# A decoder layer on one core: softmax tiles per head, output casts ahead of their remainders, sines moved into the query round, and other places for w_in's and w_out's products

## The chip, the cores and the metric

The kernel runs on one core of a Trainium2 chip. The metric is the time of one execution on the device, in microseconds (us), as the median of several runs. The profile shows one further execution, whose own time is given beside its span.

## What is computed

The reference is one step of a hybrid decoder layer, in float32, for a prompt of 272 positions (16 meta tokens and 256 tokens) and 8 sample tokens that share the weights (`T` = 280 columns in all). Cut to what matters:

```python
h = rmsnorm(x, norm_mix_g)
z = h @ w_in                                   # 2048 -> u 1024 | q 1024 | k 256 | v 256
q = rope(rmsnorm(q, q_norm_g), pos); k = rope(rmsnorm(k, k_norm_g), pos)
# SSM: 64 groups of 16 channels, 64 complex states each
x_re, x_im = coef * (u @ b)                    # complex product per group
s = associative_scan(a, x)                     # s[t] = a * s[t-1] + x[t]
y = gelu(Re(s @ c) + d_skip * u);  y = y * sigmoid(y @ w_glu + b_glu)
# attention: 16 query heads on 4 key heads of 64, window 128, softmax with a sink per head
o = softmax([q @ k.T * 64**-0.5 | sink])[..., :-1] @ v   # prompt in blocks of 128;
                                               # each sample token against its 128 cached keys and itself
x = x + [rmsnorm(y) | rmsnorm(o)] @ w_out
x = x + (silu(gate) * val) @ w_down            # val, gate = conv3(rmsnorm(x) @ w_up), 5632 channels each
```

The outputs are the layer's result, the last 128 keys and values, the last SSM state, and the last rows of the convolution. The a of the scan needs a cosine and a sine of lam_im x dt, and the kernel also needs the cosines and sines of its multiples by the position within a chunk: these are the tiles `csT` and `snT`.

## The kernel before

Every product with a weight matrix is made as three products (`mm3`, L232 to L235): the weights and the activations are split into a high part in a shorter format and the remainder, and wh x xh, wh x xl and wl x xh add up in one accumulator `acc`. Weights come in blocks of 512 KB on SP's DMA queue (`wload`, L207 to L210, three buffers `w`). `wsplit` (L212) makes the two parts: ACT casts `wh` (L216), DVE subtracts `wl` (L72). Both have two buffers and go ahead of other work that is ready (`high_priority`), so the cast of block n waits until PE is done with block n - 2, and stands in ACT's order wherever the scheduler put it.

PE's order is the order of the program text; a scheduler sets the order of the other engines when the kernel is built. All engines run their instructions in that fixed order, and an engine whose next instruction waits does nothing else. The order of the program is made of generators that are advanced one step at a time with `next`:

- The query round (L747 to L753): 16 steps of `qs_`, half of a query product each (q1 to q8; q8a and q8b are the halves of the last). Between them run steps of `kv_chain` (keys) and of `prm`, which prepares the parameters of the SSM on DVE. The squares of each query product (`sqr_s`, L640, ACT) are summed by PE (`qss`, L724).
- `q_norm`, then the attention rounds i = 1 to 8 (L1016 to L1034). Each prompt group (`att_group`, L833 to L890; 4 key heads in blocks A, then B) has three steps: scores on PE (`sps`) and the softmax on DVE and ACT (maximum, exponentials `P`, L861, sum, reciprocal, scaled `P`, L867); transposes of P on PE (`ppt`, L875) and their copies `pt`; and the product with v (`ops`, L884) with `att_out` (L806 to L822), which writes the attention output as a cast `ah` (ACT, L814) and a remainder `al` (DVE, L815), and its squares `osqt` (ACT). I number them `sps0` to `sps7`, and `ppt` and `ops` likewise.
- Between the steps of the groups stand halves of the products for u (`us`, named U1, U2 and so on here; 24 matmuls each), steps of the attention of the meta tokens (`att_meta`: `mps`, `mtp`, `mop`) and of the sample tokens (`att_sample`, L892 to L955: `ssp` twice, `osp`, `otp`). Two tables say how many stand where in each round: `UD` for the halves of u (before the `ppt` of the round, after it, after `ops`), and `SD` for steps of meta and sample (before `ppt`, after `ops`); `side` (L1006) takes meta first.
- In the sample attention the cached keys come in four tiles `KT` of 256 KB on SP's queue (L901), with three buffers; POOL copies the new key into each (L902). `ssp1` reads the first two, `ssp2` the other two.
- Before round 1, `prm_trig` makes `csT` and `snT` on ACT in four slices: an `Abs` (L451), a cosine (L452) and a sine (L453) each.

Behind the rounds stands the loop over eight state-space units, with halves of w_out's products (`oas`, 12 matmuls each) between its steps. Unit i is prepared by `ssm_in` (`lps`, L1082 to L1090), its taps by `ssm_fir`; then `vps` (L1115), the rotation `z`, `q` on DVE with `csT` and `snT`, the scan (L1129) with the factors `d0`, and the output `yps`. `d0` (L1061) is made once, from `mg4` and `mask`. The sums of squares of the attention output (`ors_`: `orps`, then a reciprocal square root on DVE, then `dg` and a second `orps`, which spreads it over the partitions) scale what w_out gives for the attention half (`oas<-acc,ors`). The gate of the SSM, the rest of w_out and the convolutional FFN follow; from 345 us on the FFN's products run one behind the other.

Of the kernel before, what the change touches and what calls it, by code (L numbers as in the profile page):

```python
# [65 lines left out]
def body(ctx, tc, I, O, dbg=None):  # L66
# [132 lines left out]

    UD = ((1, 1, 0), (2, 1, 0), (1, 1, 0), (0, 2, 0), (0, 1, 1), (1, 1, 0), (0, 1, 0), (0, 0, 0))  # L200

    SD = ((1, 0), (1, 1), (1, 1), (1, 1), (1, 1), (1, 0), (0, 1), (1, 1))

# [67 lines left out]
    def run(g):  # L271
        for _ in g:
            pass
# [316 lines left out]
    sp = pool(ssm_ctx, "ssm", "right")  # L590
    SO = sp.tile([128, 2, 9, 32], F32, name="SO")
    csT = sp.tile([128, 32, 80], F32, name="csT")
# [4 lines left out]
    ah0 = sp.tile([128, 2, 32, 8], F32, name="ah0")  # L597
    mask = sp.tile([128, SC_], F32, name="mask")
    sdp = sp.tile([128, 8], F32, name="sdp")
    V.memset(mask, 1.0)  # L600
    V.memset(mask[:, 0:1], 0.0)
    V.memset(mask[:, NCH:SC_], 0.0)
    G.tensor_copy(sdp, vsl("ssm_d"))
# [140 lines left out]
    for f in range(4):  # L744
        A.copy(kvr[:, f, :], kv_ps[f])
    kvc = kv_chain()
    for i in range(16):  # L747
        next(qs_)
        if i < 2:
            next(rs1)  # L750
        if i > 0:
            next(kvc, None)
        if i >= 2:  # L753
            slices(prm, 1)
    run(kvc)
    run(prm)
# [52 lines left out]
    def att_out(f, src, c, n):  # L809

        m = src.shape[1]
        for a in range(m):
            g = vcol("attn_out_g", f + a)
            A.activation(ah[:, f + a, c:c + n], src[:, a], AF.Copy, scale=g)  # L814
            V.scalar_tensor_tensor(al[:, f + a, c:c + n], src[:, a], g, ah[:, f + a, c:c + n].bitcast(F32),  # L815
                                   op0=OP.mult, op1=OP.subtract)
        z = small.tile([128, T], F32, name="osqt", tag="tb")[:, :m * n].rearrange("p (a b) -> p a b", a=m)
        A.activation(z, src, AF.Square)
        o = osq[:, c:c + n]
        if f == 0:  # L820
            add(o, z[:, 0], z[:, 1], eng=G)
        for a in range(2 if f == 0 else 0, m):  # L822
            add(o, o, z[:, a], eng=G)
# [11 lines left out]
    def att_group(nm, kv):  # L835
# [22 lines left out]
        add(se, sk, nm_)  # L858
        P = aw.tile([128, 4, 256], F32, name="P", bufs=1)
        for r in range(4):  # L860
            A.activation(P[:, r, :nk], sps[:, r % 2, r // 2, :nk], AF.Exp, scale=sc[:, r:r + 1], bias=nm_[:, r:r + 1],  # L861
                         accum_out=den[:, r:r + 1])
# [3 lines left out]
        for r in range(4):  # L866
            A.activation(P[:, r, :nk], P[:, r, :nk], AF.Copy, scale=rec[:, r:r + 1])  # L867
        hp.__exit__(None, None, None)
# [4 lines left out]
        for bi, (c, n, vv) in enumerate(blocks):  # L873
            for r in range(4):
                PE.transpose(ppt[:n, bi, r, :], P[:, r, c:c + n], ident)  # L875
        for bi, (c, n, vv) in enumerate(blocks):
# [128 lines left out]
    def side(k):  # L1005
        for _ in range(k):  # L1006
            if next(mg, 1) == 1:
# [3 lines left out]
                   oa_evac(f), step=4, hold=True) for f in range(16)]  # L1011
    trig = prm_trig()
    slices(trig, 4)
    next(gs_[0])
    next(us)
    next(gs_[0])  # L1016
    for i in range(1, 9):
        if i < 8:
            next(gs_[i])
        for _ in range(UD[i - 1][0]):  # L1020
            next(us)
        side(SD[i - 1][0])
        next(gs_[i - 1])
        if i < 8:
# [4 lines left out]
        if i == 8:  # L1029
            run(mg)  # L1030
            run(sg)
            next(oas[0])
        next(gs_[i - 1])
# [19 lines left out]
    for t in (*C0s, *kzs):  # L1053
        G.memset(t, 0.0)
    SO4 = SO.rearrange("p c b r -> p c r b")
    Li, U2, FIR, lpk = {}, {}, {}, {}
# [120 lines left out]
    ssm_load(0)  # L1177
    next(oas[0])
    ssm_in(0)
    next(oas[1])  # L1180
    next(ors_)
    ssm_load(1)
# [276 lines left out]
```

## Time and profile before

| | |
|---|---|
| median of 3 runs | 1163.37 us (1162.06 to 1163.4) |
| the profiled execution's own time | 1162.89 us |
| its span, from the first to the last instruction | 1161.1 us |
| mean granted clock of TensorE | 0.991 |
| PE busy | 1119.5 us (96% of the span), 9479 instructions |
| DVE busy | 807.0 us (69%) |
| ACT busy | 584.7 us (50%) |
| POOL busy | 88.2 us (8%) |
| HBM | 204 MB moved, 176 GB/s over the span |

Busy time is a sum over the whole span. The engine PE is the array of TensorE, DVE VectorE, ACT ScalarE, POOL GpSimd, and SP issues DMAs. In a timeline a row is one instruction or a run of like ones: start, length, engine, line, what it writes and reads, how many, and in brackets how long the engine had been idle before it and what ended the idle time. A tile's name stands without its number. A granted clock of 1.00 is TensorE's upper level (2.4 GHz), 0.50 the lower (1.2 GHz).

### The profile page before, as it was taken

The numbers are of one execution on the slowest core, as the hardware profiler recorded it, in microseconds if no ns is written. First come the engines' busy times: TensorE is split into PE (matmuls) and PEld (weight loads), VectorE is DVE, ScalarE is ACT, GpSimd is POOL, SyncE is SP. The second block draws the span as 40 slices with busy tenths as digits, with TensorE's granted clock in tenths as the row PEclk, the third lists the DMA queues.
The fourth block names the chain that finished last, engine by engine and source line by source line (L and its number), as shares of the span: only waits on it lengthen the run. The fifth ranks groups of instructions, "written<-read, shape, count | busy, mean of one in ns | idle before, by whom it ended". The sixth has DMA issues, their size and how long they took to land.

```text
span 1161.1 us, 23509 instructions
## 1 busy us (share of the span) xinstructions
PE 1119.5 (96%) x9479; PEld 1081.7 (93%) x9479; DVE 807.0 (69%) x1471; ACT 584.7 (50%) x961; POOL 88.2 (8%) x224
## 2 busy tenths in 40 slices
PE   7998997889989999999999999999999999999998
PEld 6887876778889999999999999999999999999998
DVE  8698995998789667677676544456776667664443
ACT  5668677554646455445444433334455445443332
POOL 1020121000142000010000000000000000000000
PEclk9999999999999999999999999999999999999999
DMA  8546465454556556666665555555555555556663
GB/s 282 145 126 174 128 185 156 117 164 122 161 159 181 177 182 184 188 193 191 183 187 182 174 175 186 184 184 174 178 182 178 173 176 182 181 189 199 193 203 125
DMA packets 237020, 203.29 MB, mean 175 GB/s; under 512 B 15960, under 2 KB 231912, under 8 KB 236904
## 3 DMA queue, kind: packets, MB, share of 16 engines
q1 hardware_dynamic: 233344, 195.26, 54.8%
q10 hardware_dynamic: 2608, 3.57, 0.9%
q0 software_dynamic: 960, 2.98, 0.9%
q8 instruction: 74, 1.21, 0.5%
q14 instruction: 34, 0.28, 0.1%
HBM read 195.96 MB, written 8.25 MB: 176 GB/s over the span
## 4 chain that ended last, share of the span: by engine, by line
PE 88%; DVE 6%; ACT 3%; DMA 2%; issue 1%; SPq 0%; ACTq 0%; DVEq 0%
PE acc L233 27%; PE acc L235 27%; PE acc L234 27%; DVE wl L72 2%; PE kvb L572 1%; DMA yd<-ysb 1%; ACT wh L216 1%; PE ops L884 1%; PE ppt L875 1%; DMA yr<-yd 1%; DVE z L1129 0%; PE sps L846 0%; DVE q L72 0%; DMA KT<-ck_t 0%; PE kvb L234 0%
## 5 line engine op out<-in xcount | busy, mean ns | idle before, releaser
L72 DVE TENSOR_TENSOR wl<-w,wh 128x1024 fp32r<-128x1024 f32 (+1 forms) x348 | 419.2, 1205 | 303.4 <-ACT wh L216 298.6
L216 ACT CAST wh<-w 128x1024 fp32r<-128x1024 f32 (+1 forms) x348 | 358.2, 1029 | 490.3 <-PE acc L234 331.3
L233 PE MATMUL acc<-x2h,wh 128*128 128x266 f32 x1408 | 397.0, 287 | 0.7 <-DVE os L72 0.7
L234 PE MATMUL acc<-x2l,wh 128*128 128x266 f32 x1408 | 395.7, 286 | 0.0
L235 PE MATMUL acc<-x2h,wl 128*128 128x266 f32 x1408 | 375.0, 287 | 0.0
L234 PEld LDWEIGHTS acc<-x2l,wh 128*128 128x128 f32 x1408 | 267.1, 190 | 0.1
L233 PEld LDWEIGHTS acc<-x2h,wh 128*128 128x128 f32 x1408 | 265.9, 189 | 0.9 <-issue 0.9
L235 PEld LDWEIGHTS acc<-x2h,wl 128*128 128x128 f32 x1408 | 254.2, 189 | 0.1
L234 PE MATMUL acc<-hl,wh 128*128 128x264 f32 x704 | 196.1, 284 | 0.0
L233 PE MATMUL acc<-hh,wh 128*128 128x264 f32 x704 | 196.0, 284 | 0.0
L235 PE MATMUL acc<-hh,wl 128*128 128x264 f32 x704 | 184.2, 284 | 0.0
L234 PEld LDWEIGHTS acc<-hl,wh 128*128 128x128 f32 x704 | 132.3, 188 | 0.0
L233 PEld LDWEIGHTS acc<-hh,wh 128*128 128x128 f32 x704 | 132.3, 188 | 0.0
L235 PEld LDWEIGHTS acc<-hh,wl 128*128 128x128 f32 x704 | 126.1, 188 | 0.0
L233 PE MATMUL acc<-xh,wh 128*128 128x266 f32 (+1 forms) x256 | 77.6, 303 | 0.0
L235 PE MATMUL acc<-xh,wl 128*128 128x266 f32 (+1 forms) x256 | 75.1, 293 | 2.2 <-DVE wl L72 2.1
L234 PE MATMUL acc<-xl,wh 128*128 128x266 f32 (+1 forms) x256 | 74.6, 292 | 0.0
L1334 POOL COPY coll<-up 128x10 f32<-128x10 f32 x88 | 17.1, 194 | 625.9 <-DVE up L72 625.8
L233 PEld LDWEIGHTS acc<-xh,wh 128*128 128x128 f32 x256 | 49.2, 192 | 4.2 <-issue 3.4
L235 PEld LDWEIGHTS acc<-xh,wl 128*128 128x128 f32 x256 | 48.8, 191 | 3.2 <-DVE wl L72 3.1
L234 PEld LDWEIGHTS acc<-xl,wh 128*128 128x128 f32 x256 | 49.2, 192 | 0.1
L1337 ACT ACTIVATE ct<-up,cin 128x256 f32<-128x256 f32 x88 | 48.1, 594 | 0.0
(365 smaller groups left out, 1424.8 us busy)
## 6 DMA issues: line engine op xcount, KB each, us to landing
w<-w_up SPq DMA_DIRECT2D x176, 512.0 KB
w<-w_down SPq DMA_DIRECT2D x64, 512.0 KB
w<-w_in SPq DMA_DIRECT2D x40, 512.0 KB
w<-w_out SPq DMA_DIRECT2D x32, 512.0 KB
w<-w_down SPq DMA_DIRECT2D x32, 384.0 KB
w<-w_glu SPq DMA_DIRECT2D x8, 512.0 KB
U<-ud SPq DMA_DIRECT2D x16, 168.0 KB
buf<-x_t SPq DMA_DIRECT2D x4, 532.0 KB
```

What stands on the lines that cost most here:

```text
L72: return eng.tensor_tensor(o, a, b, op=op)
L216: A.copy(wh[:, :nk, :], w[:, :nk, :])
L233: PE.matmul(ps, wh, xh, start=st, stop=False)
L234: PE.matmul(ps, wh, xl, start=False, stop=False)
L235: PE.matmul(ps, wl, xh, start=False, stop=sp)
L572: PE.matmul(kv_ps[f], kw[b][:, j, cc], xs[:, b + j, :], start=b + j == 0, stop=False)
L875: PE.transpose(ppt[:n, bi, r, :], P[:, r, c:c + n], ident)
L884: PE.matmul(ops[64 * par:64 * par + 64], vv[:n, 64 * kv:64 * kv + 64], pts[bi][:n, par::2, :], start=bi == 0, stop=bi == 1)
L1334: G.tensor_copy(coll[:, n, :], up[:, NR - 10:NR])
L1337: A.activation(t, up[:, 2:258], AF.Identity, scale=cin[:, n, 2:3], bias=cin[:, n, 3:4])
```

## The change

The change does seven things.

1. The exponentials of a group go into one tile per head, from a ring of seven, instead of one tile for four heads.
2. `att_out` makes all casts `ah` of a group before the first remainder `al`.
3. The four slices of `prm_trig` run in the last four steps of the query round instead of before round 1.
4. `UD` and `SD` give other places to the halves of u and to the steps of meta and sample.
5. In round 8 the rest of meta and sample and the first half of w_out's first product stand before `ppt7`, and its second half before `ops7`.
6. In the SSM's beginning the first `orps` stands before `ssm_in(0)`, and no half of w_out between.
7. `SO` and `mask` come from a later pool; POOL fills the mask after the rounds, where DVE filled it before them.

```diff
-    UD = ((1, 1, 0), (2, 1, 0), (1, 1, 0), (0, 2, 0), (0, 1, 1), (1, 1, 0), (0, 1, 0), (0, 0, 0))
+    UD = ((1, 1, 0), (2, 1, 0), (1, 1, 0), (0, 1, 0), (1, 1, 0), (1, 1, 0), (1, 1, 0), (0, 0, 0))
-    SD = ((1, 0), (1, 1), (1, 1), (1, 1), (1, 1), (1, 0), (0, 1), (1, 1))
+    SD = ((1, 1), (1, 1), (1, 1), (1, 1), (1, 1), (1, 1), (1, 1), (0, 0))
...
-    mask = sp.tile([128, SC_], F32, name="mask")
-    V.memset(mask, 1.0)
...
+    mask = sw.tile([128, SC_], F32, name="mask", bufs=1)
+    G.memset(mask, 1.0)
...
-    kvc = kv_chain()
+    kvc, trig = kv_chain(), prm_trig()
     for i in range(16):
...
+        if i >= 12:
+            slices(trig, 1)
...
         for a in range(m):
+            A.activation(ah[:, f + a, c:c + n], src[:, a], AF.Copy, scale=vcol("attn_out_g", f + a))
+        for a in range(m):
             g = vcol("attn_out_g", f + a)
-            A.activation(ah[:, f + a, c:c + n], src[:, a], AF.Copy, scale=g)
             V.scalar_tensor_tensor(al[:, f + a, c:c + n], src[:, a], g, ah[:, f + a, c:c + n].bitcast(F32),
                                    op0=OP.mult, op1=OP.subtract)
...
-        P = aw.tile([128, 4, 256], F32, name="P", bufs=1)
+        P = [aw.tile([128, 256], F32, name="P", bufs=7) for _ in range(4)]
...
-    trig = prm_trig()
-    slices(trig, 4)
     next(gs_[0])
...
+        if i == 8:
+            run(mg)
+            run(sg)
+            next(oas[0])
         next(gs_[i - 1])
...
         if i == 8:
-            run(mg)
-            run(sg)
-            next(oas[0])
+            next(oas[1])
         next(gs_[i - 1])
...
     next(oas[0])
+    next(ors_)
     ssm_in(0)
-    next(oas[1])
-    next(ors_)
     ssm_load(1)
```

What this makes of the order of the engines is shown at three places.

ACT, from the end of the query round to the first exponentials of the attention (round 1). `wh` is the cast of a weight block, `sqr_s` the squares that `qss` waits for, `csT` and `snT` the cosines and sines, `acc` with a number the query product that is read. Before:

```order
L640 ACTIVATE sqr_s<-acc_982 128x266
L634 COPY rope_s<-acc_982 32x266 x4
L702 COPY buf<-buf 64x280 x4
L216 CAST wh<-w 128x1024 x2
L640 ACTIVATE sqr_s<-acc_1077 128x266
L634 COPY rope_s<-acc_1077 32x266 x4
L708 COPY vx<-ksp 8x256
L216 CAST wh<-w 128x1024 x2
L640 ACTIVATE sqr_s<-acc_1170 128x266
L634 COPY rope_s<-acc_1170 32x266 x4
L451 ACTIVATE csT<-snT 128x640 x4
L452 ACTIVATE csT<-csT,cvec 128x640
```

Further on in the same order, where the last sine and the first exponentials stand:

```order
L216 CAST wh<-w 128x1024
L452 ACTIVATE csT<-csT,cvec 128x640
L453 ACTIVATE snT<-snT 128x640
L216 CAST wh<-w 128x1024
L861 ACT_TABLE_LOAD
L861 ACTIVATE P,st<-sps,st,rq 128x144 x4
L863 ACTIVATE st<-st 128x4
L216 CAST wh<-w 128x1024
L867 ACTIVATE P<-P,st 128x144 x2
```

With the change:

```order
L451 ACTIVATE csT<-snT 128x640 x2
L697 COPY buf<-buf 64x280 x4
L452 ACTIVATE csT<-csT,cvec 128x640
L453 ACTIVATE snT<-snT 128x640
L452 ACTIVATE csT<-csT,cvec 128x640
L453 ACTIVATE snT<-snT 128x640
L216 CAST wh<-w 128x1024 x2
L635 ACTIVATE sqr_s<-acc_1072 128x266
L629 COPY rope_s<-acc_1072 32x266 x4
L703 COPY vx<-ksp 8x256
L451 ACTIVATE csT<-snT 128x640 x2
L452 ACTIVATE csT<-csT,cvec 128x640
```

Further on in the same order:

```order
L216 CAST wh<-w 128x1024 x2
L635 ACTIVATE sqr_s<-acc_1171 128x266
L629 COPY rope_s<-acc_1171 32x266 x4
L216 CAST wh<-w 128x1024 x3
L859 ACT_TABLE_LOAD
L859 ACTIVATE P,st<-sps,st,rq 128x144 x7
L861 ACTIVATE st<-st 128x4 x2
L976 ACTIVATE mS<-mS 2x256
L865 ACTIVATE P<-P,st 128x144 x4
```

Two slices of cosines and sines have moved ahead of the two casts for q8a and q8b (the first `x2`), and two ahead of the next two casts, for U1 and U2, behind which the squares of q8 stand. Three casts, for U3 to U5, now stand together ahead of the table load, where the third stood between exponentials and scaled P, and seven exponentials follow one another.

PE, in round 4, around the sample scores (`ssp`; the first two rows are `ops2`). Before, `ssp1` was followed by `ppt3`, two halves of u and `ops3` before the second `ssp` came. With the change:

```order
L882 MATMUL ops<-pt,vx 64x256 x2
L882 MATMUL ops<-pt,vA 64x256 x2
L907 MATMUL ssp<-KT,Qf 32x128 x8
L840 LDWEIGHTS identb
L840 MATMUL sps<-maskB,identb 128x512
L840 LDWEIGHTS identb
L840 MATMUL sps<-maskB,identb 128x512
L844 MATMUL sps<-buf 128x256 x4
L907 MATMUL ssp<-KT,Qf 32x128 x8
L873 MATMUL ppt<-ident,P 16x128 x4
L873 MATMUL ppt<-ident,P 128x128 x4
```

Only the scores of the next group (`sps`) stand between the two.

DVE, at the beginning of the state-space loop: `rs_v`, `rs_r` and `rq_t` are the steps of the reciprocal square root that follows the first `orps`, `z` and `q` the rotation of unit 0. Before, these steps stood one behind the other:

```order
L72 TENSOR_TENSOR rq_t<-rs_v,rs_r 128x3
L172 SCALAR_TENSOR_TENSOR rq_t<-rq_t,rs_r 128x3
L173 SCALAR_TENSOR_TENSOR rs_r<-rq_t,rs_r 128x3
L72 TENSOR_TENSOR rq_t<-rs_v,rs_r 128x3
L172 SCALAR_TENSOR_TENSOR rq_t<-rq_t,rs_r 128x3
L173 SCALAR_TENSOR_TENSOR rs_r<-rq_t,rs_r 128x3
L72 TENSOR_TENSOR dg<-ident,rs_r 128x384
L72 TENSOR_TENSOR wl<-w,wh 128x1024
L72 TENSOR_TENSOR z<-vps,csT 128x608
L72 TENSOR_TENSOR q<-vps,snT 128x608
L72 TENSOR_TENSOR oas<-acc_2461,ors 128x266
L72 TENSOR_TENSOR oas<-acc_2583,ors 128x266
```

With the change:

```order
L72 TENSOR_TENSOR rq_t<-rs_v,rs_r 128x3
L72 TENSOR_TENSOR wl<-w,wh 128x1024
L172 SCALAR_TENSOR_TENSOR rq_t<-rq_t,rs_r 128x3
L72 TENSOR_TENSOR z<-vps,csT 128x608
L72 TENSOR_TENSOR q<-vps,snT 128x608
L173 SCALAR_TENSOR_TENSOR rs_r<-rq_t,rs_r 128x3
L72 TENSOR_TENSOR z<-z,q 128x304 x2
L72 TENSOR_TENSOR dg<-ident,rs_r 128x384
```

`dg` has moved behind the rotation, which reads `vps`, and the reciprocal square root is spread among it.

## Rows read from the trace of the kernel before

**Rows 1.** Windows by stage: us from:to, length, busy us (instructions) of each engine, PEclk, DMA.

```profile
98.00:210.00 112.00, 101.02 (x856) 82.57 (x855) 92.83 (x243) 83.47 (x215) 19.96 (x40) 0.97 0.56 156
210.00:280.00 70.00, 61.35 (x1022) 54.12 (x1022) 66.04 (x117) 35.35 (x84) 4.97 (x16) 0.95 0.49 131
```

**Rows 2.** Waits of PE, 90 to 206 us: total us, times, longest us.

```profile
PE ppt L875 <- ACT P L867: 5.4, 2, 3.6
PE qss L724 <- ACT sqr_s L640: 1.3, 1, 1.3
PE acc L233 <- ACT ah L814: 0.9, 1, 0.9
PE otp L949 <- ACT oV L943: 0.8, 1, 0.8
PE acc L235 <- DVE wl L72: 0.5, 1, 0.5
PE acc L233 <- ACT ah L829: 0.5, 1, 0.5
```

**Rows 3.** Timeline of ACT: start us, length, line, operation, idle before and releaser.

```profile
88.34 1.05 ACT L216 CAST wh<-w 128x1024 fp32r<-128x1024 f32 x1
...
98.28 1.04 ACT L216 CAST wh<-w 128x1024 fp32r<-128x1024 f32 x1 [2.40 <-PE acc L234]
...
101.20 2.62 ACT L451 ACTIVATE csT<-snT 128x640 f32<-128x640 f32 x4
103.73 0.81 ACT L452 ACTIVATE csT<-csT,cvec 128x640 f32<-128x640 f32 x1
...
105.07 0.82 ACT L452 ACTIVATE csT<-csT,cvec 128x640 f32<-128x640 f32 x1
...
111.11 1.28 ACT L861 ACT_TABLE_LOAD   x1
112.41 0.47 ACT L861 ACTIVATE P<-sps,st,rq 128x144 f32<-128x144 f32 x1
...
114.22 0.21 ACT L863 ACTIVATE st<-st 128x4 f32<-128x4 f32 x1
...
115.28 0.72 ACT L867 ACTIVATE P<-P,st 128x144 f32<-128x144 f32 x2
```

**Rows 4.** Timeline of PE, the places that the change touches.

```profile
91.45 0.37 PE L233 MATMUL acc<-xh,wh 128*128 128x266 f32 x1
...
100.23 0.40 PE L233 MATMUL acc<-xh,wh 128*128 128x280 f32 x1
...
113.38 0.56 PE L963 MATMUL mps<-buf 64*2 64x16 f32 x32
115.74 2.24 PE L875 MATMUL ppt<-ident,P 128*16 128x128 f32 x8 [1.81 <-ACT P L867]
...
148.15 1.04 PE L875 MATMUL ppt<-ident,P 128*16 128x128 f32 x8
...
156.46 0.64 PE L909 MATMUL ssp<-KT,Qf 128*32 128x128 f32 x16
...
158.64 1.80 PE L875 MATMUL ppt<-ident,P 128*128 128x128 f32 x8
...
183.00 2.50 PE L875 MATMUL ppt<-ident,P 128*128 128x128 f32 x8 [3.57 <-ACT P L867]
```

**Rows 5.** Timeline of POOL, the copy into the last cache tile.

```profile
152.95 0.19 POOL L902 COPY KT<-buf 128x4 f32<-128x4 f32 x1 [0.33 <-DMA KT<-ck_t]
```

**Rows 6.** Timeline of DVE, behind the first `vps`.

```profile
206.48 0.56 DVE L72 TENSOR_TENSOR dg<-ident,rs_r 128x384 f32<-128x384 f32 x1
206.96 1.22 DVE L72 TENSOR_TENSOR wl<-w,wh 128x1024 fp32r<-128x1024 f32 x1
208.10 0.78 DVE L72 TENSOR_TENSOR z<-vps,csT 128x608 f32<-128x608 f32 x1
```

**Rows 7.** Windows, granted clock behind `ppt0`.

```profile
116.00:118.00 2.00, 1.96 (x9) 1.43 (x9) 2.00 (x7) 0.70 (x3) 0.00 (x0) 0.50 0.93 273
```

More of the change, by code (lines that the diff above doesn't have):

```diff
@@ L590, in body @@
     sp = pool(ssm_ctx, "ssm", "right")
-    SO = sp.tile([128, 2, 9, 32], F32, name="SO")
     csT = sp.tile([128, 32, 80], F32, name="csT")
@@ L597, in body @@
     ah0 = sp.tile([128, 2, 32, 8], F32, name="ah0")
-    mask = sp.tile([128, SC_], F32, name="mask")
     sdp = sp.tile([128, 8], F32, name="sdp")
-    V.memset(mask, 1.0)
-    V.memset(mask[:, 0:1], 0.0)
-    V.memset(mask[:, NCH:SC_], 0.0)
     G.tensor_copy(sdp, vsl("ssm_d"))
@@ L858, in att_group @@
         add(se, sk, nm_)
-        P = aw.tile([128, 4, 256], F32, name="P", bufs=1)
+        P = [aw.tile([128, 256], F32, name="P", bufs=7) for _ in range(4)]
         for r in range(4):
-            A.activation(P[:, r, :nk], sps[:, r % 2, r // 2, :nk], AF.Exp, scale=sc[:, r:r + 1], bias=nm_[:, r:r + 1],
+            A.activation(P[r][:, :nk], sps[:, r % 2, r // 2, :nk], AF.Exp, scale=sc[:, r:r + 1], bias=nm_[:, r:r + 1],
                          accum_out=den[:, r:r + 1])
@@ L866, in att_group @@
         for r in range(4):
-            A.activation(P[:, r, :nk], P[:, r, :nk], AF.Copy, scale=rec[:, r:r + 1])
+            A.activation(P[r][:, :nk], P[r][:, :nk], AF.Copy, scale=rec[:, r:r + 1])
         hp.__exit__(None, None, None)
@@ L874, in att_group @@
             for r in range(4):
-                PE.transpose(ppt[:n, bi, r, :], P[:, r, c:c + n], ident)
+                PE.transpose(ppt[:n, bi, r, :], P[r][:, c:c + n], ident)
         for bi, (c, n, vv) in enumerate(blocks):
@@ L1054, in body @@
         G.memset(t, 0.0)
+    SO = sw.tile([128, 2, 9, 32], F32, name="SO", bufs=1)
+    mask = sw.tile([128, SC_], F32, name="mask", bufs=1)
+    G.memset(mask, 1.0)
+    G.memset(mask[:, 0:1], 0.0)
+    G.memset(mask[:, NCH:SC_], 0.0)
     SO4 = SO.rearrange("p c b r -> p c r b")
```

## The prediction

> **What bounds the kernel now.** I read first the windows by stage. In the attention (98 to 210 us) PE has work for 101.0 of 112 us and DVE for 92.8; in the state-space loop behind it (210 to 280) DVE is busy 66.0 of 70 us and PE 61.4 [rows 1]. So the change is decided on PE's idle places up to the loop, and at the loop by when DVE can start. Second, PE's waits by releaser between 90 and 206 us: two waits of the transposes `ppt` for the scaled P (5.4 us, longest 3.6), one of `qss` (1.3), and four of 0.5 to 0.9 [rows 2]. Third, the timelines of ACT, PE and DVE at these places. After each of the two `ppt` waits PE ran slower: the granted clock was 0.50 at 116 to 118 us, the lower level, 1.2 GHz [rows 7], and `ppt6` took 2.50 us where `ppt3` took 1.04 [rows 4]; with the matmuls behind it that was about 2.3 us. All sums are made against the profiled execution (1162.89 us), 0.5 under the median of the runs.
>
> **What goes.** The wait of `ppt6` (3.57) with its slow stretch (2.3), that of `otp` (0.8), and the two for `ah` (0.9 and 0.5) [rows 2, 4] hang on ACT standing behind DVE: the second cast of `ah` waited for `al` of the first, and ACT's next work stood behind that cast. With all casts first, the wait on DVE is gone from ACT, and U units now stand ahead of `ppt6`. I count 8.1 us removed there and 0.5 left over.
>
> **Sines in q's round (ACT).** Abs costs 2.62 for four slices, a pair of sines 1.34 (103.73 to 105.07) [rows 3]. A lot of two slices is 1.31 + 2 x 1.34 = 4.0 us. The first lot now stands ahead of the cast for q8a, which began at 88.34: 92.3, and q8a's first product comes at 93.35 instead of 91.45 [rows 3, 4]; its third product waits for DVE's split behind that cast, another 0.85 (a split takes 1.22 [rows 6]). The cast of U2 waits for q8b's end (98.28 in the trace, after an idle of 2.40), and the squares that `qss` needs stand behind that cast, so the delay goes through: U1 starts at about 103.4 instead of 100.23 [rows 3, 4]. **+3.2.** Bounds: 0, if ACT's idle takes all 8.0, to 5.6, if only the 2.40 does.
>
> **Round 1 (ACT).** The sines no longer stand in front of the exponentials, which should help: they began at 112.41 [rows 3]. But three casts of weights now stand ahead of the table load, for U3, U4 and U5, and with two buffers the third waits for PE's end of U3. That end was 113.38 (where `mps` begins); 3.2 later, less the 0.5 that U3 lost to `wl` and some 0.3 of closer packing, it is 115.75 [rows 2, 4]. Behind it: cast 1.0, table load 1.28, four exponentials 1.81 (112.41 to 114.22), three of the next group (1.36, for P now has seven buffers, so they need not wait), and from the sum over DVE to the first scaled P some 1.1 to 1.7 (the trace has 1.06 from the small exponential to the first scaled P at 115.28, with a cast between; the larger value has `mS` ahead) [rows 3]. `ppt0` starts at 123 instead of 115.74, after an idle of 6.6 instead of 1.81, and is followed by the lower clock in both kernels [rows 4, 7]. U4 is late by 7.1: **+3.9** more. Bounds of that step: -2.3 (its own waits of 1.81 and 0.5 vanish) to +5.
>
> **Rounds 2 and 3.** The same work in the same order of engines, no row with a wait: 0, covered by U units; if that cover went, the nearest wait is 0.5 [rows 2].
>
> **Round 4 (PE, SP, POOL).** The second half of the sample scores, `ssp2`, moves from behind `ppt3`, two U units and `ops3` to directly behind `sps4`. Its fourth cache tile has the buffer of the first and is loaded only when `ssp1` is done, at 148.15, where `ppt3` begins; POOL, waiting for that transfer, copies into it at 152.95 for 0.19 [rows 4, 5], so `ssp2` can end its wait 5.0 us after `ssp1`. The trace's `ssp2` came at 156.46 and never waited [rows 4]. Now only `sps4` (2.18 for `ssp2` and `sps5` together, so 1.6) lies between: PE idles 3.4, in round figures **+3.3**. Bounds: 1 (the transfer at its quickest, some 2.5) to 3.3 + 2.3 with a slow stretch as after `ppt6`. By the Trainium skill, "DMA: Bandwidth & Descriptors", section "Anatomy of one DMA", a transfer takes about 2.0 us and its bytes over 436 GB/s, an estimate of 2.6 us for this tile of 262 KB (the fit is for transfers that GpSimd issues); the trace has 4.8 from `ssp1` to the copy and disagrees, and by the page the total would be 2.2 us lower.
>
> **Round 5.** DVE's maximum over `ssp` waits for that late `ssp2`, and the reciprocal for `ppt4` stands behind it. `ppt4` took 1.80 where 1.04 is usual, so it waited 0.8 inside [rows 4]; I take 2.0: **+1.2**, between 0 and 3.3.
>
> **Casts first, buffers per head, masks.** The casts cost ACT nothing new. P in separate tiles lets `ppt` start on the first scaled head instead of the fourth, under 1.1 us (three copies of 0.36 [rows 3]) and only where `ppt` waits; that is in the 123 above. The mask's three fills move from DVE to POOL, which has room, 0; but the product d0 that reads them moves on DVE from an idle place to behind the last `al`. The time PE takes up to `vps` covers it; if not, up to 2.9 us of d0 come on top.
>
> **The end.** `orps` now stands right behind the second half of w_out's first product, before `lps`. It needs squares that ACT makes behind the same casts; the nearest rows are the two `ah` waits there, 0.9 + 0.5: **+1.4**, between 0 and 3.6. The product of `orps` with `dg` comes right after `vps`; in the trace DVE had made `dg` from 206.48 on, ahead of `z` and `q` [rows 6]. Now `dg` stands behind `z`, `q` (0.78 each) and the difference of both, which themselves wait for `vps`: 3 x 0.78 + 0.56 and some small steps, 3.2 us of PE idle, and 0.3 more at the next w_out product. I cost these 3.5 at nothing: they come after `vps`, DVE works on meanwhile, and PE has 8.6 us of idle in the loop [rows 1]. If that cover is gone, +3.5.
>
> **Sum.** At `vps`, from the bold terms and the stretch at `ppt6`: 3.2 + 3.9 + 3.3 + 1.2 - 8.1 + 0.5 + 1.4 = +5.4. Behind it DVE sets the pace and has 4.0 us of idle in 70 [rows 1], which may take between 0 and 4.0 of the lag; I take 0.8, since most of DVE's idle there is waiting for transfers that come later by the same lag. **+4.6**: 1167.5 for the profiled execution, 1168.0 against the median.
>
> **Rivals.**
> - *The exponentials find their place* (faster). Place: ACT in round 1. With the sines out of the way and seven P buffers, the exponentials run while PE is in U3, and `ppt0` doesn't wait. Then the walk's 6.6 of idle and the slow stretch (about 2.1) are gone: 4.6 - 8.7 = -4.1; with the sines hidden in ACT's idle as well, up to -7.3. Time 1156 to 1159.3, say 1157.5. It decides itself by whether ACT's third cast is past before U3 ends. For it: ACT is busy 83.5 of 112 us [rows 1]; the stall is long and depends on one instruction's place. Against it: ACT runs in order, and the cast waits for a buffer that only U3's end frees. Chance 0.25.
> - *Nothing to measure.* The new waits are as large as the old, and the loop takes the rest (4.0 of absorption, or a quicker cache tile): +4.6 - 3.2 - 1 = about 0.4, so 1163.8. Chance 0.15.
> - *Slow clock on top* (slower still). The idle of 3.3 before `ssp2` is as long as the 3.57 before `ppt6`, which was followed by the lower level; +2.3, and the `dg` wait without cover +3.5: 1170.3 to 1173.8. The short idles in q's round (1.9 and 0.85) may add one as well. Chance 0.15.
>
> **How the numbers follow.** The forecast has 0.45, its own range 1165.8 (that is, 2.2 us lower, with a quicker cache tile) to 1170. About 0.2% (2.3 us) is what a measurement of this kernel can tell from no change. Faster takes the first rival, 0.25; same the second, 0.15; slower the forecast and the third, 0.60. For 8 in 10 the range runs from 1157.0, inside the first rival, to 1173.0, inside the last.
>
> **What would show it.** In the profile after: the cast ahead of q8a near 92 and U1 near 103.4; ACT's table load behind a cast that waited for PE, and `ppt0` near 123 with an idle over 5 us; `ssp2` waiting 2 to 4 us for POOL's copy of the cache tile; no wait at `ppt6`; `orps` waiting about 3 us for DVE's `dg`; the loop's last rows later by 4 to 5 us. The forecast is wrong if `ppt0` waits under 3 us, or if the loop begins no later than before although these waits are there.

## The result and the profile after

| | before | with the change |
|---|---|---|
| median | 1163.38 us (4 runs) | 1178.41 us (4 runs, 1174.83 to 1180.42) |
| ratio | | 1.012, 95% interval 1.0105 to 1.0135 |
| the profiled execution's own time | 1162.89 us | 1179.86 us |
| its span | 1161.1 us | 1178.1 us |
| mean granted clock | 0.991 | 0.983 |
| PE busy | 1119.5 us (96%) | 1125.5 us (96%) |

The change makes the kernel 15 us slower: the direction was forecast, the size was three times the 4.6 us of the sum and lies outside the range. Between the two profiled executions it is 17.0.

PE's waits by releaser in the changed kernel, 90 to 231 us (total us, times, longest):

```profile
PE ppt L873 <- ACT P L865: 8.3, 2, 6.9
PE orps L193 <- DVE dg L72: 3.9, 1, 3.9
PE orps L185 <- POOL osq L72: 2.7, 1, 2.7
PE ssp L907 <- POOL KT L900: 2.5, 1, 2.5
PE acc L233 <- ACT wh L216: 1.7, 1, 1.7
PE qss L719 <- ACT sqr_s L635: 1.6, 1, 1.6
...
PE orps L185 <- issue: 0.6, 1, 0.6
```

The waits for `otp` and `ah` of [rows 2] are gone; one wait at `ppt0` is longer than all of the old ones at `ppt`, and `ssp` and `orps` are new. The same kernel's windows (columns as in [rows 1]; the first two are the stretches of [rows 1] moved by 11 us, the others are places behind a wait):

```profile
98.00:221.00 123.00, 107.02 (x852) 89.14 (x854) 91.42 (x237) 77.40 (x204) 17.92 (x43) 0.90 0.52 147
221.00:291.00 70.00, 57.97 (x989) 50.16 (x982) 65.69 (x118) 35.96 (x89) 3.67 (x14) 0.95 0.47 124
...
124.00:128.00 4.00, 3.94 (x17) 3.29 (x18) 3.97 (x15) 3.05 (x11) 0.00 (x0) 0.51 0.01 2
160.00:166.00 6.00, 6.00 (x33) 5.42 (x28) 2.82 (x8) 1.05 (x2) 3.67 (x7) 0.55 0.24 64
174.00:178.00 4.00, 3.49 (x15) 2.92 (x16) 3.97 (x9) 3.64 (x13) 0.00 (x0) 0.71 0.79 255
214.00:220.00 6.00, 5.30 (x36) 4.77 (x37) 1.91 (x11) 1.17 (x4) 0.64 (x1) 0.50 0.38 111
224.00:228.00 4.00, 2.79 (x22) 1.74 (x22) 3.97 (x8) 0.44 (x2) 0.00 (x0) 0.50 0.40 116
```

The clock column is what the prediction had looked at in one place only. The mean granted clock is 0.90 before the loop (0.97 in [rows 1]), and the lower level stands behind the four longest waits and behind `ppt4`'s 1.42. DVE is no busier in the loop than before (65.7 of 70 us).

PE at the places that the steps are about, in the changed kernel:

```profile
104.26 0.39 PE L233 MATMUL acc<-xh,wh 128*128 128x280 f32 x1
...
124.06 1.30 PE L873 MATMUL ppt<-ident,P 128*16 128x128 f32 x4 [6.88 <-ACT P L865]
...
159.36 1.07 PE L907 MATMUL ssp<-KT,Qf 128*32 128x128 f32 x12 [2.47 <-POOL KT L900]
160.35 1.88 PE L873 MATMUL ppt<-ident,P 128*16 128x128 f32 x8
...
174.30 1.97 PE L873 MATMUL ppt<-ident,P 128*128 128x128 f32 x6 [1.42 <-ACT P L865]
...
214.70 1.01 PE L185 MATMUL orps<-ones,osq 128*128 128x1 f32 x4 [2.70 <-POOL osq L72]
...
220.56 0.76 PE L1118 MATMUL vps<-U,Li 64*64 64x76 f32 x32
225.21 1.65 PE L193 MATMUL orps<-dg,ones 128*128 128x384 f32 x2 [3.89 <-DVE dg L72]
...
240.08 0.62 PE L1101 MATMUL lps<-ident,kz 128*64 128x128 f32 x4 [1.17 <-DVE kz L72]
```

And the rows of the kernel before that answer to the last ones and were not among [rows 4], the first `vps`, the product with `dg`, and the third `kz`:

```profile
206.24 0.76 PE L1115 MATMUL vps<-U,Li 64*64 64x76 f32 x32
207.10 0.91 PE L193 MATMUL orps<-dg,ones 128*128 128x384 f32 x2
...
222.64 0.63 PE L1098 MATMUL lps<-ident,kz 128*64 128x128 f32 x4 [1.92 <-DVE kz L72]
```

Against [rows 4]: U1 is 4.0 late, `ppt0` 8.3 (its idle is 6.88 instead of 1.81), `vps` 14.3, the third `kz` of the loop 17.4, and so is the end, to half a microsecond. ACT at the end of the query round and in round 1:

```profile
93.07 1.98 ACT L216 CAST wh<-w 128x1024 fp32r<-128x1024 f32 x2
...
101.39 1.97 ACT L216 CAST wh<-w 128x1024 fp32r<-128x1024 f32 x2
...
116.59 1.04 ACT L216 CAST wh<-w 128x1024 fp32r<-128x1024 f32 x1 [3.20 <-PE acc L234]
117.66 1.28 ACT L859 ACT_TABLE_LOAD   x1
```

The order worked as the prediction walked it: the cast at 93.07 (92.3 was forecast) for q8a, the third of the late casts at 116.59, just when PE is done with U3, then the table load and seven exponentials. POOL (the copy into the cache tile, and its sums of squares) and DVE (d0, a split, `z`, and `dg`):

```profile
159.12 0.18 POOL L900 COPY KT<-buf 128x4 f32<-128x4 f32 x1 [3.05 <-DMA KT<-ck_t]
...
208.04 0.90 POOL L72 TENSOR_TENSOR osq<-osq,osqt 128x128 f32<-128x128 f32 x2 [4.22 <-ACT osqt L816]
...
211.63 3.02 POOL L72 TENSOR_TENSOR osq<-osq,osqt 128x128 f32<-128x128 f32 x2 [1.62 <-ACT osqt L816]
```

```profile
210.33 2.69 DVE L72 TENSOR_TENSOR d<-mg,mask 128x2432 f32<-128x2432 f32 x1
212.94 1.43 DVE L72 TENSOR_TENSOR wl<-w,wh 128x1024 fp32r<-128x1024 f32 x1
...
224.61 0.55 DVE L72 TENSOR_TENSOR dg<-ident,rs_r 128x384 f32<-128x384 f32 x1
```

POOL needed 3.02 us for two sums of squares beside d0 and the split, where the two before took 0.90.

### The profile page after: what moved, and what is told of

Same layout as the page of the kernel before. It is cut to its first block, busy times and chain, and to the rows that moved or that the text cites. A ratio compares the mean times of both kernels' runs of the same rounds, so it can differ in the third digit from the quotient of the medians.

```text
span 1178.1 us, 23515 instructions
## 1 busy us (share of the span) xinstructions
PE 1125.5 (96%) x9479; PEld 1087.1 (92%) x9479; DVE 808.1 (69%) x1468; ACT 583.9 (50%) x961; POOL 84.7 (7%) x227
## 3 DMA queue, kind: packets, MB, share of 16 engines
q10 hardware_dynamic: 2608, 3.57, 0.9%
## 4 chain that ended last, share of the span: by engine, by line
PE 86%; DVE 6%; ACT 3%; DMA 3%; issue 1%; POOL 0%; SPq 0%; ACTq 0%; DVEq 0%
PE acc L233 27%; PE acc L235 26%; PE acc L234 26%; DVE wl L72 2%; PE kvb L572 2%; ACT wh L216 1%; DMA yd<-ysb 1%; DMA yr<-yd 1%; PE ppt L873 1%; PE ops L882 1%; DMA w<-w_in 1%; DVE z L1132 1%; PE sps L844 1%; DVE q L72 0%; DVE S L72 0%
```

## The experiments

A new row of the program changes what the scheduler does elsewhere, so each kernel was read in its own trace. Kernels named "casts-first" and the like are built up from the kernel before; the others take parts out of the changed one. Times are medians; the kernel before had 1162.91 to 1163.38 in these comparisons, 1163.0 below.

**The sines back in round 1** (changed kernel otherwise; this edit and those below are shown in part, `...` stands for lines left out).

```diff
-        if i >= 12:
-            slices(trig, 1)
...
+    trig = prm_trig()
+    slices(trig, 4)
     next(gs_[0])
```

> The changed kernel with the sines in round 1 again. Theory (the new waits add up and reach the end): the first half of U starts near 100.2 instead of 104.3 (4.0 less), only two casts stand ahead of the table load, so ppt0 waits under 2 us instead of 6.88 (another 4.3 less); in all 8 us less, about 1170. Rival (PE's delay at the start is made up behind it, or taken by the next wait): ppt0 comes earlier, but the loop's vps stays within 2 us of 220.6, and the time is 1176 to 1180.

1168.8 us (5 runs, ratio to before 1.0068, 1.004 to 1.0096): 9.6 less than the change. `ppt0` in it:

```profile
116.84 2.25 PE L871 MATMUL ppt<-ident,P 128*16 128x128 f32 x8 [3.11 <-ACT P L863]
```

It begins at 116.84, 7.2 earlier than with the change; `vps` (211.44) comes 9.1 earlier, and the median is 9.6 lower. The theory holds in its main point, nothing made the delay up; only the wait is not under 2. The rest of it, 3.11 instead of 1.81 in [rows 4], is put down to the ring of seven, which lets exponentials of the next group go ahead of the scaled P: with a ring of four, in the run with d0 early below, `ppt0` waits 1.78.

**The sines alone** (kernel before otherwise).

> The kernel before with the sines in the query round, and nothing else. Theory (the sines cost the same wherever the rest stands): the first half of U starts near 104, ppt0 waits 5 us or more behind the third cast, and the time is 1171 to 1173. Rival (the cost needs the ring of seven P buffers, which puts more exponentials ahead): ppt0 comes near 120 and the time is 1166 to 1169.

1170.64 us (ratio 1.0064, 1.0048 to 1.008), 7.6 more than before.

```profile
122.44 2.15 PE L877 MATMUL ppt<-ident,P 128*16 128x128 f32 x8 [5.37 <-ACT P L869]
```

The wait is the theory's, the time a little under its range. The move of the sines costs nearly as much alone: the three casts ahead of the table load are its work, the ring's three more exponentials come on top.

**The old tables** (changed kernel otherwise).

```diff
-    UD = ((1, 1, 0), (2, 1, 0), (1, 1, 0), (0, 1, 0), (1, 1, 0), (1, 1, 0), (1, 1, 0), (0, 0, 0))
+    UD = ((1, 1, 0), (2, 1, 0), (1, 1, 0), (0, 2, 0), (0, 1, 1), (1, 1, 0), (0, 1, 0), (0, 0, 0))
-    SD = ((1, 1), (1, 1), (1, 1), (1, 1), (1, 1), (1, 1), (1, 1), (0, 0))
+    SD = ((1, 0), (1, 1), (1, 1), (1, 1), (1, 1), (1, 0), (0, 1), (1, 1))
```

> The changed kernel with the old tables UD and SD. Theory: the second ssp comes behind ops3 and doesn't wait for the cache tile (2.5 us and about 2.4 of low clock behind it), ppt4 doesn't wait 1.4 (and 2.6 of low clock); the old wait at ppt6 does not return, since the casts come first; 7 to 9 us less, about 1170. Rival: it was the tables that removed the wait at ppt6 (a half of U stands between sps7 and ppt6); it returns with 3.6 and 2.3 of low clock, and the time is 1174 to 1178.

1176.75 us (ratio 1.0123, 1.0102 to 1.0144), 1.7 less. The time is in the rival's range, but its mechanism is not there: `ppt6` does not wait, as the theory had it. Nor does `ssp`; but now

```profile
PE otp L947 <- ACT oV L941: 2.2, 1, 2.2
PE acc L233 <- ACT ah L827: 1.4, 1, 1.4
```

stand in the list. The new tables moved waits; by themselves they cost between -1.5 (next run) and 1.7.

**The sines and the tables back** (the edits of the first and the third run on the changed kernel).

> The changed kernel without its sines and its tables (both as before); casts first, seven P buffers, round 8, orps order and mask stay. Theory (sines cost 9.6 whatever else; the tables cost about 2): 1176.8 - 9.6 = 1167, slower than before by 3 to 5 us, which are the waits of orps for the squares (2.6) and dg (4.0) with low clock. Rival (sines and tables only cost together, and without them the casts' gain is seen): 1158 to 1162.

1170.28 us (ratio 1.0055, 1.004 to 1.007): 1.5 more than with the sines back alone. Both numbers of the theory were too low, as it took the tables for a cost of 2; the rest of the change costs 7 by itself.

**Round 8 as before** (changed kernel otherwise).

```diff
         side(SD[i - 1][0])
-        if i == 8:
-            run(mg)
-            run(sg)
-            next(oas[0])
         next(gs_[i - 1])
...
         if i == 8:
-            next(oas[1])
+            run(mg)
+            run(sg)
+            next(oas[0])
...
     ssm_in(0)
+    next(oas[1])
     ssm_load(1)
```

> The changed kernel with round 8 as before (rest of meta and sample, and the first half of w_out's first product, behind ppt7; two halves of w_out behind the first lps). dg then stands ahead of z and q on DVE. Theory: orps waits no longer for dg (3.9 us less), and orps's first product still waits for the squares (about 2.7); 4 to 6 us less, 1173 to 1174. Rival (that wait lies beside DVE's work in the loop, as the prediction had it): vps comes as early or late as before and the time is within 1.5 us of 1178.4.

1179.28 us (ratio 1.0142, 1.0123 to 1.0162), 0.9 more. The wait for `dg` vanished, as expected, but `vps` came at 223.25 instead of 220.56. Half of that is there at `ops4` already (182.24 instead of 180.84; `ssp2` waits 3.4 for its tile instead of 2.5), and 1.5 is the half of w_out that had covered `ppt7` and now stands between `orps` and `vps`. A miss for the theory. This run doesn't show the wait to be hidden, though; it is replaced by work and other waits.

**The first `orps` behind `ssm_in(0)` again** (changed kernel otherwise).

```diff
     next(oas[0])
-    next(ors_)
     ssm_in(0)
+    next(ors_)
     ssm_load(1)
```

> The changed kernel with the first orps behind ssm_in(0) again; dg then stands even further behind z and q on DVE. Theory: the wait of orps for POOL's squares (2.7) goes, as lps covers it, but the wait for dg grows by 2 to 4 us, as the steps of the reciprocal square root wait behind more; 0 to 2 us less or as much more, 1177 to 1180. Rival (the first orps is what costs, and dg is hidden): 3.3 us less, 1175.

1178.21 us (ratio 1.0132, 1.0111 to 1.0153), 0.2 less.

```profile
214.04 0.60 PE L185 MATMUL orps<-ones,osq 128*128 128x1 f32 x4 [2.48 <-POOL osq L72]
...
216.60 0.76 PE L1118 MATMUL vps<-U,Li 64*64 64x76 f32 x32
225.43 1.65 PE L193 MATMUL orps<-dg,ones 128*128 128x384 f32 x2 [8.07 <-DVE dg L72]
```

The wait for `dg` grew to 8.1, as expected, but that for POOL's squares did not go: POOL was late by itself, not PE early. Two things more stand in these rows. Behind the wait of 2.48 the clock stayed at 1.00 (214 to 218 us), and `vps` came 4.0 earlier than with the change; but the product with `dg` came when it had (225.43, 225.21), and nothing was won. In this run DVE's steps, not PE's, set the time at that place.

**The casts first, alone** (kernel before otherwise).

```diff
         for a in range(m):
+            A.activation(ah[:, f + a, c:c + n], src[:, a], AF.Copy, scale=vcol("attn_out_g", f + a))
+        for a in range(m):
             g = vcol("attn_out_g", f + a)
-            A.activation(ah[:, f + a, c:c + n], src[:, a], AF.Copy, scale=g)
```

> The kernel before with the casts of the attention output first, and nothing else. Prediction's step: ACT no longer stands behind DVE's remainder; the waits at ppt6 (3.6, with 2.3 of low clock), otp and ah are gone; 4 to 8 us less than before, 1156 to 1159. Rival (ACT waits there for DVE's maximum and other work anyway, so that the wait keeps its size under another name): within 1.5 us of before.

1161.48 us (10 runs, ratio 0.998, 0.9967 to 0.9994), 1.5 less. PE's waits and the window of the attention rounds:

```profile
PE ppt L876 <- ACT P L868: 4.1, 2, 2.4
PE otp L950 <- ACT oV L944: 2.2, 1, 2.2
...
102.00:180.00 78.00, 72.44 (x611) 60.95 (x611) 73.06 (x197) 58.48 (x150) 17.06 (x27) 0.98 0.54 151
```

`ppt6` no longer waits, but `ppt3` waits 2.35 and `otp` 2.20. DVE is busy 73.1 of 78 us in these rounds; in the kernel before it was 73.5. The step failed here: the casts opened a place, and the next one closed. (The profiled execution took 1158.88, 2.6 under the median. A part of that is the clock: it was 1.00 behind `ppt0`, at 116 to 120 us, where the kernel before had 0.57 behind an idle as long, 1.79 and 1.81 us.)

**The same with one half of U moved** from behind `ppt3` to before it, and **with a step of the sample attention moved as well**.

```diff
-    UD = ((1, 1, 0), (2, 1, 0), (1, 1, 0), (0, 2, 0), ...
+    UD = ((1, 1, 0), (2, 1, 0), (1, 1, 0), (1, 1, 0), ...
...
-    SD = ((1, 0), (1, 1), (1, 1), (1, 1), (1, 1), (1, 0), (0, 1), (1, 1))
+    SD = ((1, 0), (1, 1), (1, 1), (1, 1), (1, 1), (1, 1), (0, 1), (1, 1))
```

> The casts-first kernel (1161.5) with one half of U moved from behind ppt3 to before it (the part of the table that the change has at that place, too). Theory: ppt3's wait of 2.35 and the slow stretch behind it (about 2) go, and ssp2 still has 5 us from ssp1; 1157 to 1160, faster than both kernels. Rival (the wait moves to another transposes, as it did with filling): 1161 to 1164.

> As the last, with one step of the sample attention moved to the end of round 6, so that otp stands further behind osp. Theory: otp's wait of 2.2 goes as well, another 1 to 3 us less, 1155 to 1159. Rival: DVE's and ACT's work for the earlier step delays the softmax of the last groups, and nothing is won over the last.

1162.53 us (12 runs, ratio 0.9992, 0.9979 to 1.0004), and 1161.13 (12 runs, 0.9976, 0.9963 to 0.9988). In the first, `ppt3` waits no more, and the old wait is back at `ppt6`:

```profile
PE ppt L876 <- ACT P L868: 5.7, 2, 3.9
```

So the rival holds. The second is the fastest kernel of the study with the casts-first one; the two can't be told apart, and both beat the kernel before, by 1.5 and 1.8 us, less than was expected.

**d0 early** (the changed kernel with the sines back, `SO` and `mask` in their old place, four P buffers).

```diff
+    mask = sp.tile([128, SC_], F32, name="mask")
+    V.memset(mask, 1.0)
...
-    mask = sw.tile([128, SC_], F32, name="mask", bufs=1)
-    G.memset(mask, 1.0)
...
-        P = [aw.tile([128, 256], F32, name="P", bufs=7) for _ in range(4)]
+        P = [aw.tile([128, 256], F32, name="P", bufs=4) for _ in range(4)]
```

> The changed kernel with the sines in round 1, and with SO and mask in their old place, which leaves room for four P buffers only (still one tile per head). The product d0 then stands ahead of the last remainders on DVE, and dg ahead of z and q. Against the run with the sines back alone (1168.8): theory (d0 on DVE beside POOL's two sums of squares makes these take 3.0 instead of 0.9, and holds up dg): orps's wait for the squares falls from 2.6 to under 1 and that for dg (3.7) goes; 3 to 6 us less, 1163 to 1166. Rival (the ring of seven is needed): ppt waits grow, and the time is 1168 or more.

1165.55 us (10 runs, ratio 1.002, 1.0009 to 1.0032): 3.3 less than with the sines back alone. POOL's sums of squares and DVE's d0 in it:

```profile
199.69 2.94 POOL L72 TENSOR_TENSOR osq<-osq,osqt 128x128 f32<-128x128 f32 x2 [4.58 <-ACT osqt L819]
...
204.72 0.90 POOL L72 TENSOR_TENSOR osq<-osq,osqt 128x128 f32<-128x128 f32 x2 [1.23 <-ACT osqt L819]
```

```profile
199.17 2.69 DVE L72 TENSOR_TENSOR d<-mg,mask 128x2432 f32<-128x2432 f32 x1 [0.55 <-DMA ud<-uu]
```

The two sums that run beside d0 (and a pair of remainders) take 2.94, the two that come when DVE is idle 0.90. `orps` waits 0.6 for the squares, and not at all for `dg`. The waits and the time are the theory's, but not all of the way there: the slowed pair is the earlier one now, behind it POOL fills `C0b`, a tile of the loop, ACT waits 1.27 for that, and the last squares begin 1.2 later than with the sines back alone (204.19, 202.97). `orps` is idle 1.6 ahead of its first products instead of 0.6, and `vps` comes no earlier (211.93, 211.44). The gain lies behind `vps`, where `dg` no longer waits: the third `kz` is 3.2 earlier (227.73, 230.96). The edit changes the ring as well; the next run has the mask alone.

**The late mask on the casts-first kernel**, and **the order of round 8 and `orps` on it**: the change's part 7, and its parts 5 and 6. The core of each:

```diff
-    V.memset(mask, 1.0)
...
+    mask = sw.tile([128, SC_], F32, name="mask", bufs=1)
+    G.memset(mask, 1.0)
```

```diff
+        if i == 8:
+            run(mg)
+            run(sg)
+            next(oas[0])
         next(gs_[i - 1])
...
     next(oas[0])
+    next(ors_)
     ssm_in(0)
```

> The casts-first kernel with SO and mask from the later pool. d0 then stands on DVE behind the last remainder, and dg behind z and q. Theory (late d0 holds up POOL's squares and dg): orps waits 2 us or more for the squares and 3 or more for dg, 4 to 6 us more than the casts-first kernel, 1165 to 1167. Rival (PE's idle in the loop covers them, as the prediction had it): within 1.5 us of 1161.5.

> The casts-first kernel with round 8 and the first orps as in the change; mask, P, tables and sines as before. d0 stays early. Theory (the order by itself costs little when d0 is early): orps waits under 1.5 us and dg under 1, 1161 to 1164. Rival (the order is what costs at the end): orps waits 2.5 us or more, 1165 to 1168.

1163.96 us (10 runs, ratio 1.0007, 0.9995 to 1.002), 2.5 more than the casts-first kernel: `orps` waits 1.0 for the squares and 3.1 for `dg`, where the casts-first kernel waits 0 and 1.6; half of what was expected. And 1166.01 us (10 runs, ratio 1.0024, 1.0014 to 1.0034), 4.5 more, although the waits of `orps` are as small as the theory had them and `dg` has none. In the two profiled executions the stretch from `otp` to `vps`, with the same work, is 6.7 longer than in the casts-first kernel (19.1 and 12.4 us). Where it went, from the waits and the windows of the second:

```profile
PE acc L233 <- ACT ah L830: 1.4, 1, 1.4
...
PE orps L185 <- POOL osq L72: 0.6, 1, 0.6
...
196.00:198.00 2.00, 2.00 (x11) 2.00 (x11) 0.00 (x0) 0.00 (x0) 0.00 (x0) 0.50 0.05 16
206.00:212.00 6.00, 6.00 (x54) 5.01 (x57) 3.29 (x15) 2.57 (x6) 0.00 (x0) 0.50 0.51 140
```

With the old tables `otp` has waited 2.2 already, then the first half of w_out waits 1.38 for casts of the sample output, which `ppt7` used to cover; and the stretches behind this wait and behind `orps` run at the lower clock. Neither expectation named that mechanism.

**`ppt0`'s idle filled.** The changed kernel with products that nobody reads:

```diff
         side(SD[i - 1][0])
+        if i == 1:
+            dm = acc.tile([128, 512], F32, name="dm", tag="acc")
+            for _ in range(24):
+                PE.matmul(dm, identb, maskb["B"][:, None, :256].to_broadcast([128, 2, 256]), start=True, stop=True)
```

> The changed kernel with 24 extra products of 512 columns (some 6.5 us) into an unused accumulator between mps and ppt0, so that PE does not idle while it waits there; their result is not read. Theory (PE's slow stretch behind ppt0 comes from the idle before it): ppt0 starts when it did, 124, takes 1.04 instead of 2.15, and the half of U behind it 3.1 instead of 4.2; 2 us less. Rival (the low clock comes from what runs there): ppt0 and U4 are as slow as they were, 0 less.

1177.1 us (ratio 1.0112, 1.0094 to 1.0131), 1.3 less. `ppt0` began at 123.87 as before, the clock stayed at 1.00, and `ops0` came at 128.52 instead of 130.02. The theory holds for this place, with 1.5. But the next wait took most of it:

```profile
158.99 1.07 PE L907 MATMUL ssp<-KT,Qf 128*32 128x128 f32 x12 [3.60 <-POOL KT L900]
```

The cache tile came hardly earlier, and `vps` at 220.21 instead of 220.56. So 0.35 of the 1.3 is explained by the rows.

**All five idles filled** in the same way: before `ppt0` (29), the second `ssp` (11), `ppt4` (6), and the two products of `orps` (14 and 17, into a tile of pool `one`).

```diff
+            if u == 1:
+                dm = acc.tile([128, 512], F32, name="dm", tag="acc")
+                for _ in range(11):
+                    PE.matmul(dm, identb, maskb["B"][:, None, :256].to_broadcast([128, 2, 256]), start=True, stop=True)
             for t in range(2):
                 for g in range(4):
```

> The changed kernel with extra products, whose result is not read, in each of PE's five long idles: before ppt0 (29), the second ssp (11), ppt4 (6), and both products of orps (14, 17). The waits themselves stay. Theory (behind each idle PE works at the lower clock, and this is the part of the loss that the prediction left out): granted clock 1.00 between 98 and 221 instead of 0.90, about 1.5 to 2 us less at each of the five places, 1169 to 1172. Rival (the waits are the whole loss; a stretch at the lower clock is taken up by the next wait): 1176 to 1178.5, as with ppt0 alone filled.

1168.95 us (8 runs, ratio 1.0046, 1.0032 to 1.0061): 9.5 less than the change. Window, `ppt0` and `vps` of it:

```profile
98.00:221.00 123.00, 118.94 (x992) 92.60 (x995) 100.22 (x255) 79.06 (x210) 21.69 (x45) 1.00 0.52 148
...
123.99 1.19 PE L873 MATMUL ppt<-ident,P 128*16 128x128 f32 x4 [0.52 <-ACT P L865]
...
210.81 0.76 PE L1127 MATMUL vps<-U,Li 64*64 64x76 f32 x32
```

The clock is 1.00 through the whole stretch. `ppt0` is where it was, since the waits in front of it are untouched; `vps` comes at 210.81, not 220.56. Of these 9.75 us, 1.3 lie between `ppt0` and `ops0`, 3.2 from `ssp1` to `ops3`, 2.7 from there to `ops4`, and 2.4 between `orps` and `vps`; some 0.7 of it are waits that came out shorter, as the cache tile came 4.25 after the beginning of `ssp1` and not 4.8. The first 1.3 are no part of the difference between the kernels: in the kernel before PE was as slow behind `ppt0` (5.96 us from `ppt0` to `ops0` in both). So 7 to 8 us are what the prediction had left out.

**Three idles of the casts-first kernel filled**, in the same way.

```diff
+        if i in FILL:
+            dm = acc.tile([128, 512], F32, name="dm", tag="acc")
+            for _ in range(FILL[i]):
...
+    FILL = {1: 7, 4: 10}
...
         otp = one.tile([128, 2, 8, 8], F32, name="otp", tag="one")
+        dm = acc.tile([128, 512], F32, name="dm", tag="acc")
+        for _ in range(9):
```

> The casts-first kernel (1161.5) with extra products, whose result is not read, in PE's idle places before ppt0 (7), ppt3 (10) and otp (9). Theory (each idle there is followed by a slow stretch that costs 0.5 to 2): clock 1.00 in these stretches and 2 to 4 us less, 1157.5 to 1159.5, which is faster than both kernels. Rival (PE's time there is taken up by the next wait): 1161 to 1163.

1163.7 us (11 runs, ratio 1.0006, 0.9997 to 1.0015): a miss. The three idles were gone and the clock behind them was 1.00, but with the fillers the scheduler ordered ACT otherwise, and `ppt6` waited 3.64 again: as the rival said, the next wait took it up.

Put one on the other, each kernel holding the parts of the one before it, the medians go so: before 1163.0; casts first 1161.5 (-1.5); round 8 and `orps` 1166.0 (+4.5); new tables and a tile per head 1165.55 (-0.5); late mask and ring of seven 1168.8 (+3.3); sines 1178.4 (+9.6). Another order of the steps would divide it otherwise: the sines alone cost 7.6, the mask alone 2.5, and the new tables between -1.5 and 1.7.

## Why the prediction was wrong

By its steps, at the first `vps` of the loop, between the two profiled executions:

| step | predicted | measured |
|---|---|---|
| sines, to U1 | +3.2 | +4.0 |
| round 1, to `ppt0` | +3.9 | +4.3 |
| second `ssp`: idle | +3.3 | +2.5 |
| the same: lower clock behind it | 0 (in a rival, 2.3) | +2.4 (`ssp2`'s end to `ops3`, 6.4 where 4.1 is usual) |
| `ppt4` | +1.2 | +3.2 (idle 1.42, slow 2.5, less the 0.75 it had) |
| `ppt6` to the third half of w_out | -7.6 | -9.0 (30.2 us from `ops4` on instead of 39.2, without the `lps` that stands there before) |
| first `orps` to `vps` | +1.4 | +5.9 (idle 0.61 + 2.70, slow 2.6) |
| sum | +5.4 | +13.3; +14.3 by the rows, 1.0 not assigned |
| `dg`, behind `vps` | 0 (cover), else 3.5 | +3.1 (third `kz`) |
| taken up by the loop | -0.8 | -0.4 |

- **What held.** The direction, the three casts ahead of the table load and what they wait for, the moment of `ppt0` (123 forecast, 124.06), the wait for the cache tile, `dg` behind `z` and `q`. The rival that the exponentials find their place fell: the third cast ended after U3. The rule of the Trainium skill, "DMA: Bandwidth & Descriptors", section "Anatomy of one DMA", would have put the tile 2.2 us earlier; the tile's copy began 4.7 us after the end of the first `ssp` before and 4.2 (154.94 to 159.12) now, where the page's fit gives an estimate of 2.6, so the trace disagrees again (the fit is for transfers that GpSimd issues, this one is issued by SP).
- **The step that failed most** is the term that was left out: the slow stretch behind a wait. The prediction said of `ppt6` that its wait of 3.57 was followed by 2.3 of lower clock and counted this as removed, but added nothing behind the waits that it forecast, except in a rival with a chance of 0.15. In the table it is 2.4 behind `ssp2`, 2.5 behind `ppt4` and 2.6 behind `orps`, 7.5 us where the sum had nothing. The run with all idles filled shows it as cause: 9.5 us less, 7 to 8 of them slow stretches at places where the kernel before was not slow. What is left of the loss in that run is 6.0 (1168.95), near the 4.6 of the sum, though the errors of the other steps partly cancel in that. The third rival had `ssp2` and `dg` nearly at the right price (2.3 and 3.5 for 2.4 and 3.1); the stretches behind `ppt4` and `orps` are in no rival.
- **The first `orps`.** It was bounded by ACT's waits; most of its idle is for POOL (2.70, and 0.61 ahead of it). d0 had been costed as covered by PE's work up to `vps`. Its cost came through POOL, whose two sums take 3.0 us beside it; the run with d0 early has `orps` waiting 0.6 for them, not 2.7, though other idle took half of that, and the run with the late mask alone has a wait of 1.0 that the casts-first kernel does not have.
- **`dg` at nothing.** The cover named was PE's idle in the loop. But the loop's first DVE steps wait for the second `lps` and `vps`, which stand behind that product in PE's order, so DVE got the delay at once (`z` of unit 1 waits 1.9 us for `vps` at 232.20). That the loop would take 0.8 failed as well: the lag at the third `kz` is 17.4 and at the end 17.0. Idle of an engine that is waiting for another that is late is no room.
- **The casts.** In the changed kernel the stretch from `ops4` on did get 9.0 shorter. The same stretch is 35.6 us with the old tables and 34.0 with the casts first alone, so the casts are 3.6 to 5.2 of the 9.0 and the new tables the most of the rest, which they lose again at `ssp2` and `ppt4`. Alone the casts are worth 1.5 in the medians: in that run's trace the stretch is 5.2 shorter, but `ops4` comes 2.4 later (165.86 instead of 163.45), behind the new wait of `ppt3`. What one `ppt` no longer waits, another does. A likely reason is that DVE, busy 73 of 78 us in these rounds, sets the pace there; that is inferred from the runs in which the wait moved from `ppt6` to `ppt3` and back, and not shown: PE is busy 72 to 75 of the same 78 us, and no run made DVE's work less.

## What to carry to other kernels

Where the rows show a lower clock behind idle places, price an idle place at its length and the slow stretch behind it, for the waits that a change adds as well as for those it removes; here the second part was as large as the first (2.4, 2.5 and 2.6 behind waits of 2.5, 1.4 and 3.3). What is won at such a place reaches the end only if the next wait doesn't take it: 0.35 of 1.5 did at `ppt0` alone. A cast that is put ahead of other work on an engine in order brings its own wait along: look at which product frees its buffer before moving anything that used to keep it back. And a wait that goes at one place is worth only what the next engine has left, so follow the gain up to the next wait, and see which engine is busy nine tenths of that stretch, before counting it.

## What the runs showed of the hardware

- Five idles of PE in the changed kernel, from 1.4 to 6.9 us, were followed by the lower level, 1.2 GHz, for several microseconds; with products that do nothing in their place the clock stayed at 1.00 over all of 98 to 221 us and the kernel was 9.5 us faster with more work on PE. The length of the idle alone does not say whether it happens: `qss` waited 1.60 us in the changed kernel, and the clock was 1.00 behind it (104 to 108 us), while `ppt4`'s 1.42 was followed by 0.71 (174 to 178 us); and with the first `orps` behind `ssm_in(0)` its wait of 2.48 was followed by 1.00 (214 to 218 us), where the 2.70 of the changed kernel was followed by 0.50. The 1.8 ahead of `ppt0` was followed by 0.57 in the kernel before and by 1.00 in the casts-first one (116 to 120 us).
- PE's busy share hides this: it is 96% in both kernels, since a slow product counts as busy.
- POOL's addition of two tiles of 128 x 128 takes 0.90 us for two, and 2.9 to 3.0 when it begins during DVE's product d0 of two operands (nine runs and the changed kernel). Where the sums began first, in the kernel before, they took 0.97, and d0 2.90 instead of 2.69. The Trainium skill, "SBUF — State Buffer", section "SBUF: two separate sides", says that the two engines share a pair of ports, that whichever of a GpSimd operation and a DVE operation with two SBUF inputs begins first holds it for the whole instruction, and that the other engine waits until then; the rows agree both ways, though no run was made for this alone.
